# A down projection in seven half-size products with its split weight sums made beforehand

## The chip, the cores and the metric

The kernel runs on one NeuronCore of a Trainium2 chip. The metric is the time of one execution on the device in microseconds (us). The engines are TensorE (PE, with PEld for its weight loads), VectorE (DVE), ScalarE (ACT), GpSimd (POOL) and SyncE (SP). Here SP issues every transfer, in one queue in order.

## The reference, cut to what matters

One layer of a diffusion backbone for 128 context tokens and 2048 latent tokens, 2176 in all, with 1024 features, in float32. After a mixer (a gated short convolution and a bidirectional mLSTM) comes the feed-forward part, which the change concerns:

```
h2 = rmsnorm(x, norm2) * (1 + scale2) + shift2
up = conv3(h2 @ w_up)                  # 2 x 2816 features, 3 taps along the grid's columns
a, gg = split(up)
u = silu(gg) * a                       # 2816 features
x = x + gate2 * (u @ w_down)           # 2816 -> 1024
y = rmsnorm(x, final_norm)
```

D_FF is 2816 = 22 x 128. The gate and the shift differ between context and latent tokens.

## The kernel before

Features lie on the 128 partitions, tokens along the free dimension. Every float32 operand of a product is split into a high part (an ACT copy to the type that TensorE multiplies, `fp32r`) and a low part (the rest, a subtraction on DVE or POOL), and a product is three matmuls: high x high, high x low, low x high, into one PSUM bank.

The **mixer** goes over the second half of the tokens first (the blocks BB: heads, `shortconv`, heads), then over the first half (BA), where products of the projections fill the gaps of the mLSTM's units (`weave`). In it, `load_w` (L101) loads a weight block into one of two buffers, ACT makes its high part and POOL its low part; `gemm` (L191) is 24 matmuls of 384 or 256 columns into one of four accumulators.

The **up projection** already works by Strassen and Winograd's scheme: two halves of the tokens (`hf`), 22 units of features (`j`), and for each unit seven products of half size instead of eight (L918 on), with sums of tokens in seven slots (`sums`, `split`) and sums of weights made per unit (`weights`). `conv` (L879) follows one unit behind. It convolves the two raw results, multiplies them to `u` and stores 128 features of it in `uD` (L907).

The **down projection** is plain. For four groups of 544 tokens and eight blocks of 128 output features, 22 x 2 x 3 matmuls of 272 columns (L1030 to L1032) gather in two PSUM banks. `load_u` (L974) loads and splits the 22 pieces of u of a group, the next group's behind the last products of this one. `load_d` (L983) loads and splits the block's weights again in each group, the high part on ACT, the low part shared by POOL and DVE. `close` (L1034) adds the bank, scaled by the gate, onto the residual x. `finish` (L997) takes the squares' sums, gets their inverse roots by a small product and a power on POOL, spreads them over the partitions by another small product, scales the eight blocks and stores them.

A layer over the program sets the order of the instructions on each engine: it may put work that is ready ahead of work that stands earlier in the code, as far as buffers allow, and it makes all waits. On the chip each engine and SP's queue keep that order, so an instruction that waits holds up all behind it.

## Time and profile before

| what | value |
|---|---|
| executions | 2618.68, 2618.84, 2621.7 us; median 2618.84 |
| span of the profiled execution | 2622.1 us |
| mean granted clock of TensorE | 0.988 |
| PE busy | 2539.1 us, 97% |
| DVE / ACT / POOL busy | 1501.3 / 1066.1 / 706.4 us |
| moved by DMA | 403.25 MB, mean 154 GB/s |
| down projection, last up product to last down product | 2062.8 to 2610.5 us |

The profiled execution's time is its span here; no other time of it is given. A group's row in the profile has the line, engine and operation, what it writes and reads, the shape, the count, then busy time and mean duration of one, and the idle time ahead of it with what ended it. Matmuls overlap in the pipeline, so a mean duration is more than the distance between two starts. A row of the timeline has the start, the time it took, the engine, the line and the operation.

### The profile page before, as it was taken

The page shows a single profiled execution, that of the slowest core. Times are in us where ns is not written, and L with a number is a line of the kernel's source. Part 1 is how long each engine was busy: PE and PEld are TensorE (multiplying, and loading weights), DVE is VectorE, ACT ScalarE, POOL GpSimd, SP SyncE. Part 2 cuts the span into 40 slices and gives each one's busy share as a digit, 9 for nine tenths or more (in the row PEclk, how much of TensorE's full clock was granted, in tenths as well). Part 3 has the DMA queues.
Part 4 walks back from the last instruction along what each step waited for, and adds up shares of the span by engine and source line. Part 5 has one row for each costly group of instructions (what it writes and reads, how often), then busy time and mean ns, then how long its engine had stood idle before and what let it go on. Part 6 is the DMA issues. An engine that isn't in the chain of part 4 may idle for free. (4 is left out here: it accounts for less than half of the span.)

```text
span 2622.1 us, 46918 instructions
## 1 busy us (share of the span) xinstructions
PE 2539.1 (97%) x18511; PEld 2519.2 (96%) x18511; DVE 1501.3 (57%) x2560; ACT 1066.1 (41%) x2028; POOL 706.4 (27%) x534
## 2 busy tenths in 40 slices
PE   8999999999988988899999999999999999999998
PEld 7999999999988988899999999999999999999998
DVE  3993242333457666797686669666666635353533
ACT  4521142322345454464454446554544523232411
POOL 2542242211333344221121112111111222232232
PEclk9999999999999999999999999999999999999999
DMA  8773142555467887854252224222222635454442
GB/s 280 250 254 101 57 140 85 155 180 155 152 195 242 253 256 235 267 195 139 84 178 91 79 79 165 83 83 82 83 83 90 234 113 184 156 179 150 149 139 77
DMA packets 223582, 403.25 MB, mean 154 GB/s; under 512 B 20722, under 2 KB 144770, under 8 KB 221698
## 3 DMA queue, kind: packets, MB, share of 16 engines
q1 hardware_dynamic: 223362, 400.25, 46.5%
q8 instruction: 145, 2.38, 0.4%
q14 instruction: 75, 0.61, 0.1%
HBM read 305.13 MB, written 95.04 MB: 153 GB/s over the span
## 5 line engine op out<-in xcount | busy, mean ns | idle before, releaser
L196 PE MATMUL acc<-hH,wh 128*128 128x384 f32 (+1 forms) x1536 | 516.4, 336 | 0.0
L198 PE MATMUL acc<-hH,wl 128*128 128x384 f32 (+1 forms) x1536 | 505.0, 329 | 0.0
L197 PE MATMUL acc<-hL,wh 128*128 128x384 f32 (+1 forms) x1536 | 504.7, 329 | 0.0
L938 PE MATMUL pa<-tH,wh 128*128 128x272 f32 x1408 | 410.1, 291 | 5.6 <-DVE raw L950 5.2
L940 PE MATMUL pa<-tH,wl 128*128 128x272 f32 x1408 | 409.3, 291 | 0.4 <-DVE wl L276 0.4
L1030 PE MATMUL d<-uh,wh 128*128 128x272 f32 x1408 | 406.0, 288 | 3.1 <-ACT raw L948 3.1
L939 PE MATMUL pa<-tL,wh 128*128 128x272 f32 x1408 | 407.1, 289 | 0.0
L1032 PE MATMUL d<-uh,wl 128*128 128x272 f32 x1408 | 406.9, 289 | 0.0
L1031 PE MATMUL d<-ul,wh 128*128 128x272 f32 x1408 | 404.4, 287 | 0.0
L276 POOL TENSOR_TENSOR wl<-st,wh 128x512 fp32r<-128x512 f32 x132 | 182.3, 1381 | 730.5 <-ACT wh L275 697.5
L108 POOL TENSOR_TENSOR wl<-wst,wh 128x512 fp32r<-128x512 f32 (+1 forms) x160 | 234.3, 1486 | 434.0 <-ACT wh L105 421.5
L196 PEld LDWEIGHTS acc<-hH,wh 128*128 128x128 f32 x1536 | 291.1, 190 | 1.5 <-issue 0.4
L197 PEld LDWEIGHTS acc<-hL,wh 128*128 128x128 f32 x1536 | 291.1, 189 | 1.0
L198 PEld LDWEIGHTS acc<-hH,wl 128*128 128x128 f32 x1536 | 290.5, 189 | 0.2 <-issue 0.2
L938 PEld LDWEIGHTS pa<-tH,wh 128*128 128x128 f32 x1408 | 266.8, 190 | 6.4 <-issue 5.7
L1030 PEld LDWEIGHTS d<-uh,wh 128*128 128x128 f32 x1408 | 266.9, 190 | 3.4 <-ACT raw L948 3.3
L939 PEld LDWEIGHTS pa<-tL,wh 128*128 128x128 f32 x1408 | 267.3, 190 | 0.0
L940 PEld LDWEIGHTS pa<-tH,wl 128*128 128x128 f32 x1408 | 266.6, 189 | 0.6 <-DVE wl L276 0.6
L1032 PEld LDWEIGHTS d<-uh,wl 128*128 128x128 f32 x1408 | 266.1, 189 | 0.1
L1031 PEld LDWEIGHTS d<-ul,wh 128*128 128x128 f32 x1408 | 265.3, 188 | 0.0
L993 POOL TENSOR_TENSOR wl<-st,wh 128x704 fp32r<-128x704 f32 x64 | 150.5, 2352 | 367.2 <-ACT wh L991 358.2
L884 DVE SCALAR_TENSOR_TENSOR tt<-raw,fw,tt 128x127 f32<-128x127 f32 (+4 forms) x264 | 245.7, 959 | 1.5 <-ACT tt L890 0.8
(215 smaller groups left out, 5031.6 us busy)
## 6 DMA issues: line engine op xcount, KB each, us to landing
st<-in_w_up SPq DMA_DIRECT2D x88, 512.0 KB, 4.4
st<-in_w_down SPq DMA_DIRECT2D x64, 704.0 KB, 4.2
wst<-in_w_in SPq DMA_DIRECT2D x48, 512.0 KB, 4.1
us<-uD SPq DMA_DIRECT2D x88, 272.0 KB, 4.4
R<-nD SPq DMA_DIRECT2D x34, 512.0 KB, 5.5
wm<-in_w_modr SPq DMA_DIRECT2D x32, 512.0 KB, 4.7
F<-tD SPq DMA_DIRECT2D x12, 1088.0 KB, 8.8
uD<-tt SPq DMA_DIRECT2D x22, 576.0 KB, 2.8
```

What stands on the lines that cost most here:

```text
L108: G.tensor_sub(wl[:, a:a + n // 2], st[:, a:a + n // 2], wh[:, a:a + n // 2].bitcast(F32))
L196: PE.matmul(acc[:, :n], w_h, hH[:, k, :n], start=(k == 0), stop=False)
L197: PE.matmul(acc[:, :n], w_h, hL[:, k, :n], start=False, stop=False)
L198: PE.matmul(acc[:, :n], w_l, hH[:, k, :n], start=False, stop=(k == KT - 1))
L276: (G if on_pool else V).tensor_sub(wl, a, wh.bitcast(F32))
L884: V.scalar_tensor_tensor(o, i, w, o, op0=ALU.mult, op1=ALU.add)
L938: PE.matmul(acc, wh[:, w], rh, start=(kk == 0 and i in (0, 1, 5)), stop=False, skip_group_check=True)
L939: PE.matmul(acc, wh[:, w], rl, start=False, stop=False, skip_group_check=True)
L940: PE.matmul(acc, wl[:, w], rh, start=False, stop=(kk == 3), skip_group_check=True)
L1030: PE.matmul(acc[b][:, :NB], wh[:, c], uh[:, q], start=(j == 0), stop=False)
L1031: PE.matmul(acc[b][:, :NB], wh[:, c], ul[:, q], start=False, stop=False)
L1032: PE.matmul(acc[b][:, :NB], wl[:, c], uh[:, q], start=False, stop=(j == FT - 1))
```

## The change

1. **Down projection.** It too is made of seven products of half size. Tokens are taken in two halves of 1024 and 1152 (`HN`), features in three groups of 8, 8 and 6 blocks (`KS` pairs), outputs in four pairs of blocks (`mp`). That gives six "supers" (`SUP`) of 4 x 7 products, each with two quarters of columns (256 or 288). Each product needs one of seven sums of u, split into `uH` and `uL` (the slots `ds`, of 2048, 1536, 2304 or 1728 columns), and one of seven sums of weights, loaded as `wd` already split.
2. **Weight sums.** `prep_down`, 24 units of work run beside the mixer, loads w_down, makes the four sums and the seven splits of each unit and stores them in `wD` (168 parts, two output buffers `pw`). `wD` is read twice, once for each half of the tokens, through five buffers `wd`.
3. **Sums of u.** `conv` keeps the u of an even unit and, with that of the odd one, makes four sums and stores seven arrays in `uD`.
4. **Residual.** `evict` adds each product's bank at once onto the residual (`accs`), scaled by the gate. Since later products add onto the same bank, a bank is read between two products that add to it.
5. **Splits of u.** `Split` loads a sum into one of two buffers (`fd`), makes the high part on ACT and the low part on DVE. The seven splits of the next super go with the last pair of the present one.
6. **Final norm.** `finish` works on 1024 tokens of the first half and twice 576 of the second.

The diff, cut to its core (the old down projection, which it removes, is printed above):

```diff
+KS = (4, 4, 3)
+HN = (1024, 1152)
...
+    uD = [dr.tile([3, 7, P, 4, n // 2], F32, name=f"uD{i}") for i, n in enumerate(HN)]
+    wD = dr.tile([3, 4, 7, P, 2, 512], F32, name="wD")
...
+    def prep_down():
+        for mp in range(4):
+            for s in range(3):
+                for k0 in range(0, KS[s], 2):
+                    n = min(2, KS[s] - k0) * P
+                    c0 = (4 * s + k0) * P
+                    st = pp.tile([P, 2, 2, 256], F32, name="pst", bufs=2)
+                    Q.dma_start(st[:, :, :, :n], I["w_down"][mp][:, :, :, c0:c0 + n])
+                    a11, a12, a21, a22 = (st[:, m, k, :n] for m in range(2) for k in range(2))
+                    yield
...
+                    def part(i, a, on_pool=False):
+                        o = pp.tile([P, 2, 256], F32R, name="pw", bufs=2)
+                        S.activation(o[:, 0, :n], a, AF.Copy)
+                        (G if on_pool else V).tensor_sub(o[:, 1, :n], a, o[:, 0, :n].bitcast(F32))
+                        Q.dma_start(wD[s, mp, i][:, :, k0 * P:k0 * P + n], o[:, :, :n].bitcast(F32))
+                    part(0, a11)
+                    s1 = add(V.tensor_add, a21, a22, "ps1")
+                    part(1, s1)
+                    yield
...
+            store(4, b21)
+            store(5, b22)
+            yield
+            tt = up.tile([P, 4, 576], F32, name="ut")[:, :, :n // 2]
+            x = [tt[:, i].rearrange("p (q t) -> p q t", q=2) for i in range(4)]
+            V.tensor_sub(x[0], b12, b11)
+            V.tensor_sub(x[1], b22, x[0])
+            yield
+            V.tensor_sub(x[2], b22, b12)
+            V.tensor_sub(x[3], b21, x[1])
+            Q.dma_start(dst[:4].rearrange("i p t -> p i t"), tt)
...
+    slot_d(6)
+    fd = open_pool("fd", 2)
+    slot_d(0)
+    wd = open_pool("wd", 5)
+    for i in ORDER[2:]:
+        slot_d(i)
...
+    todo = [Split(0, 0, i) for i in ORDER]
+    for x in todo[:2]:
+        x.load()
+    ws = [next(loads) for _ in range(4)]
+    load_x(xa, 0, 0)
+    for k, x in enumerate(todo):
+        x.high()
+        x.low()
+        if k + 2 < 7:
+            todo[k + 2].load()
+        if k == 2:
+            next(cv, None)
+    run(cv)
+    phu.close()
+    xb = open_pool("xb", 8, "left")
+    dp = open_pool("dp", 1, "left")
+    for mp in range(1, 4):
+        load_x(xb, 0, mp)
...
+    def product(hf, s, mp, i, q, w):
+        N = HN[hf] // 4
+        kind = "ababaca"[i]
+        if i in (0, 1, 5):
+            banks[kind, q] = pu.tile([P, 512], F32, name="p" + kind, bufs=3 if kind == "a" else 2)
+        acc = banks[kind, q][:, :N]
+        th, tl = ds[ORDER[i]]
+        for kk in range(KS[s]):
+            c = slice((2 * kk + q) * N, (2 * kk + q + 1) * N)
+            k = slice(kk * P, (kk + 1) * P)
+            PE.matmul(acc, w[:, 0, k], th[:, c], start=(kk == 0 and i in (0, 1, 5)), stop=False, skip_group_check=True)
+            PE.matmul(acc, w[:, 0, k], tl[:, c], start=False, stop=False, skip_group_check=True)
+            PE.matmul(acc, w[:, 1, k], th[:, c], start=False, stop=(kk == KS[s] - 1), skip_group_check=True)
+        h, blk = DST[i]
+        evict(hf, mp + 4 * h, q, blk, acc)
...
+        for mp in range(4):
+            lows = []
+            for i in range(7):
+                ws.append(next(loads, None))
+                w = ws.pop(0)
+                for q in range(2):
+                    product(hf, s, mp, i, q, w)
+                for x in lows:
+                    x.low()
+                if lows:
+                    lows = []
+                    if i + 1 < 7:
+                        todo[i + 1].load()
+                if todo and mp == 3:
+                    todo[i].high()
+                    lows.append(todo[i])
+                elif todo and mp == 2 and i > 4:
+                    todo[i - 5].load()
```

Three places show how the instructions stand. The first is ACT in the short convolution of the second half of the tokens, where `cr` and `yr` are evictions and scalings of its products and `wh` the high part of the next weights. Before:

```order
L377 ACTIVATE yr<-cr,scw 128x384
L372 ACTIVATE cr<-acc 128x384
L105 ACTIVATE wh<-wst 128x1024
L372 ACTIVATE cr<-acc 128x256
L377 ACTIVATE yr<-cr,scw 128x256
```

and in the changed kernel, with the parts `pw` of the weight sums:

```order
L318 ACTIVATE pw<-pst 128x256
L413 ACTIVATE cr<-acc 128x384
L318 ACTIVATE pw<-ps_5243 128x256
L418 ACTIVATE yr<-cr,scw 128x384
L318 ACTIVATE pw<-ps_5296 128x256
L318 ACTIVATE pw<-ps_5302 128x256
L318 ACTIVATE pw<-ps_5362 128x256
L413 ACTIVATE cr<-acc 128x256
L106 ACTIVATE wh<-wst 128x1024
```

Between two evictions now stand two to five parts; 71 of the 168 stand in this convolution, most of the others in the heads and the values that follow it.

The second is SP's queue at the end of the up projection. Before (`us` is a piece of u, `ot` the residual, `st` weights):

```order
L988 DMA st_22499<-in_w_down 128x1408
L988 DMA st_22506<-in_w_down 128x1408
L976 DMA us_22513<-uD_73 128x544
L907 DMA uD_73<-tt_22265 128x1152
L976 DMA us_22519<-uD_73 128x544
```

and in the changed kernel (`acc` is the residual, `wd` a block of weight sums, `ut` the last sums of u):

```order
L1063 DMA us_23618<-uD0_73 128x2048
L1076 DMA wd_23604<-wD_75 128x1024
L1087 DMA acc_23612<-xD_70 128x1024
L1063 DMA us_23622<-uD0_73 128x2048
L1063 DMA us_23626<-uD0_73 128x2048
L981 DMA uD1_74<-ut_23651 128x4x576
L1063 DMA us_23633<-uD0_73 128x2048
L1063 DMA us_23637<-uD0_73 128x2048
L1087 DMA acc_23664<-xD_70 128x1024
L1087 DMA acc_23674<-xD_70 128x1024
L1076 DMA wd_23676<-wD_75 128x1024
```

Rows that only repeat are left out: four `wd` stand where the first one does, and six `acc` ahead of the last row, which loads the fifth block of weights.

The third is DVE at the end of the first super, where L1115 is an eviction (the old L1037) and L1070 a low part `uL` of the next super's sums (the old L980):

```order
L1115 SCALAR_TENSOR_TENSOR acc_23674<-pb_24329,modT_85,acc_23674 128x256
L1070 TENSOR_TENSOR uL_23560<-us_24262,uH_23559 128x2048
L1115 SCALAR_TENSOR_TENSOR acc_23674<-pb_24343,modT_85,acc_23674 128x256
L1115 SCALAR_TENSOR_TENSOR acc_23672<-pa_24297,modT_85,acc_23672 128x256
L1070 TENSOR_TENSOR uL_23568<-us_24293,uH_23567 128x2048
L1115 SCALAR_TENSOR_TENSOR acc_23672<-pa_24312,modT_85,acc_23672 128x256
L1070 TENSOR_TENSOR uL_23576<-us_24358,uH_23575 128x2048
```

An eviction now waits behind a low part, which waits for its load. The seven low parts spread over the last pair of this super and the first of the next.

281 lines of the change are left out of this document (163 added, 118 removed).

## The prediction

> **What bounds the kernel now.** I read the page's totals first, then the groups by line, then the starts of single products, and last the waits around the two places where the down projection begins and ends.
>
> ```profile
> span 2622.1 us, 46918 instructions
> PE 2539.1 (97%) x18511; PEld 2519.2 (96%) x18511; DVE 1501.3 (57%) x2560; ACT 1066.1 (41%) x2028; POOL 706.4 (27%) x534
> L1030 PE MATMUL d<-uh,wh 128*128 128x272 f32 x1408 | 406.0, 288 | 3.1 <-ACT raw L948 3.1
> L1031 PE MATMUL d<-ul,wh 128*128 128x272 f32 x1408 | 404.4, 287 | 0.0
> L1032 PE MATMUL d<-uh,wl 128*128 128x272 f32 x1408 | 406.9, 289 | 0.0
> ```
>
> TensorE is busy for 97% of the span, and the down projection is 3 x 1408 = 4224 products of 272 columns that hardly wait. Their 288 ns each overlap, so the price of one is the distance between two starts. Below stand the first and last row of four quiet stretches: a stretch of the down projection (82 rows listed), of the up projection (82), and of mixer products of 256 columns (36) and 384 columns (8).
>
> ```profile
> 2109.84 0.29 PE L1032 MATMUL d<-uh,wl 128*128 128x272 f32 x1
> 2119.92 0.29 PE L1032 MATMUL d<-uh,wl 128*128 128x272 f32 x1
> 1499.72 0.29 PE L939 MATMUL pa<-tL,wh 128*128 128x272 f32 x1
> 1509.93 0.29 PE L939 MATMUL pa<-tL,wh 128*128 128x272 f32 x1
> 317.82 0.28 PE L197 MATMUL acc<-hL,wh 128*128 128x256 f32 x1
> 322.00 0.29 PE L196 MATMUL acc<-hH,wh 128*128 128x256 f32 x1
> 304.73 0.34 PE L198 MATMUL acc<-hH,wl 128*128 128x384 f32 x1
> 305.97 0.34 PE L196 MATMUL acc<-hH,wh 128*128 128x384 f32 x1
> ```
>
> That is 10.08/81 = 0.1244 us a product in the down projection, 10.21/81 = 0.1260 in the up projection, 4.18/35 = 0.1194 at 256 columns and 1.24/7 = 0.177 at 384.
>
> **Term 1, the products.** Seven products of half size instead of eight leave 3696: 1848 of 256 columns (tokens 0 to 1023) and 1848 of 288. From 272 to 384 columns the price rises by (0.177 - 0.1244)/112 = 0.00047 a column, so 288 columns cost 0.132. Low: 1848 x (0.1194 + 0.132) = 465 us. High, with the up projection's dearer rate, since the new products stand in its pattern (0.1260/0.1244 = 1.013): 471. Before: 4224 x 0.1244 = 525.5. Saved: 55 to 61; taken 58.
>
> **Term 2, the final norms.** From the last up product to the last down product:
>
> ```profile
> 2062.78 0.29 PE L940 MATMUL pa<-tH,wl 128*128 128x272 f32 x1
> 2610.48 0.14 PE d L1032
> 2062.00:2064.00 2.00, 1.07 (x9) 1.00 0.89 269
> 2064.00:2066.00 2.00, 0.00 (x0) 0.80 0.87 279
> 2066.00:2068.00 2.00, 1.87 (x8) 0.50 0.78 287
> 2070.00:2072.00 2.00, 2.00 (x11) 0.50 0.90 306
> PE d L1030 <- ACT raw L948: 3.1, 1, 3.1
> PE st L133 <- POOL fr L126: 3.9, 8, 1.0
> ```
>
> The windows' columns are: length, PE busy, products, granted clock, DMA share, GB/s. The stretch is 547.7 us, 22 more than its products. The start takes 3.1 us of idle time plus some 6.8 us at clock 0.50, half of which is lost, together 6.6. The remaining 15 lie in the norms, eight of them (two blocks in each of four groups), each with sums, a power on POOL and a spreading product back to back. The change has four pieces for the kernel's body; the order shows 24 products between the two halves of the first, so POOL's answer is there in time. I leave 3 us for them: 12 saved (9 to 14).
>
> **Term 3, the start.** The old start loaded 272 KB pieces in the order of their use. The new one splits seven sums of 128x2048 in turn through two buffers, and SP has one queue. Rows for what a piece costs:
>
> ```profile
> L257 ACT ACTIVATE tH<-F x14: 1097/1112/1129, 1574.0 to 1605.9; 128x1088 fp32r<-128x1088 f32 x14
> L258 DVE TENSOR_TENSOR tL<-F,tH x14: 1278/1284/2377, 1575.3 to 1608.0; 128x1088 fp32r<-128x1088 f32 x14
> F<-tD SPq DMA_DIRECT2D x12, 1088.0 KB, 8.8
> 2050.00:2060.00 10.00, 10.00 (x81) 1.00 0.98 340
> 2230.00:2240.00 10.00, 10.00 (x83) 1.00 0.98 356
> L1037 DVE SCALAR_TENSOR_TENSOR ot<-d,modT,ot 128x272 f32<-128x272 f32 (+2 forms) x72 | 30.4, 464 | 156.6 <-PE d L1032 156.6
> ```
>
> At 2048 columns the high part costs 2.0 us on ACT and the low part 2.3 on DVE (from 1.11 and 1.28 at 1088, nearly in proportion). Full DMA engines move about 350 GB/s, so 1 MB of sums takes 3 us and its landing 5 to 9. Counting from the last up product as 0: DVE still has the last conv's taps, and the low parts 1 and 2 end near 5 and 7; the evictions of part 0 stand behind two more taps, near 11, and part 2 adds onto their bank. The multiply, three sums and the evictions of parts 1 and 2 follow to 16.5, and low parts 3 and 4 to 19 and 21. Only then are the sums 5 and 6 issued, whose buffers these free, and behind them on SP stand six loads of residual (3.1 MB) and then the fifth block of weights, issued near 24. With its own 0.5 MB, 5.7 MB have to move from 19 on, so it lands near 19 + 5.7/0.35 = 35. Parts 4, 5 and 6 follow it at 24 x 0.12 = 2.9 us each and end at 44 instead of 7 x 2.9 = 20. That is 24 us, less the 6.6 of before, about +18. Bounds: if the weights overtake, only the DVE chain is left, 12 - 6.6 = +5; with 3 us of half clock more, +22.
>
> **Term 4, five changes of token sums.** Each of the next five groups needs seven splits while TensorE works. The nearest row is the up projection's own change of halves, seven splits of about the same size in seven stages:
>
> ```profile
> 1590.00:1600.00 10.00, 9.59 (x77) 9.37 (x76) 9.06 (x11) 5.46 (x9) 1.23 (x1) 1.00 1.01 341
> 1600.00:1610.00 10.00, 9.12 (x71) 8.68 (x69) 9.89 (x12) 9.02 (x15) 2.05 (x1) 1.00 0.43 164
> 1610.00:1620.00 10.00, 8.00 (x61) 7.81 (x62) 10.00 (x17) 3.60 (x6) 3.79 (x3) 1.00 0.45 164
> 1400.00:1600.00 200.00, 199.59 (x1584) 199.37 (x1583) 142.57 (x220) 103.82 (x178) 38.38 (x27) 1.00 0.29 98
> ```
>
> Here 77 + 71 + 61 products stand where 3 x 82 would (the quiet rows above): 37 x 0.126 = 4.7 us lost. In the new phase DVE has less else to do (two evictions of 0.46 us in a step of 2.9), but a split waits for its own load, which waits for the low part two before it, and the order puts evictions behind low parts. A pair goes round in about 7 (landing) + 2.0 + 2.3 = 11.3 us against three steps of 2.9 = 8.7; three rounds fall 8 us behind, and the order has already set the last low parts into the next group's steps, which covers 4 to 6. I take 3.2 each: +16. Bounds 0 (cover holds) and 30 (the 4.7 and one landing later).
>
> **Term 5, the weight sums in the mixer.** Added: 24 loads of w_down, and 168 parts, each an ACT copy, a DVE subtraction and a store of 256 KB, plus 96 DVE sums. In all some 52 MB. The order moves most of it into the short convolution of the second half of the tokens, where the engines are idle:
>
> ```profile
> 260.00:320.00 60.00, 60.00 (x379) 60.00 (x378) 12.73 (x20) 9.83 (x15) 10.25 (x8) 1.00 0.19 60
> 320.00:380.00 60.00, 60.00 (x417) 60.00 (x416) 24.53 (x49) 30.12 (x64) 26.84 (x26) 1.00 0.45 145
> L239 ACT ACTIVATE tH<-F 128x272 fp32r<-128x272 f32 x12 | 5.0, 423 | 1.9 <-DVE F L233 1.7
> L240 DVE TENSOR_TENSOR tL<-F,tH 128x272 fp32r<-128x272 f32 x12 | 6.4, 530 | 0.0
> sD<-sb SPq DMA_DIRECT2D x32, 258.0 KB, 2.6
> xD<-row SPq DMA_DIRECT2D x40, 192.0 KB, 3.1
> ```
>
> Busy time there is no issue: 168 x 0.42 = 71 us on ACT, 264 x 0.53 = 140 on DVE, inside some 350 us. The two output buffers are: a part's buffer is free when its store has landed, so two parts take 0.42 + 0.53 + 0.2 (hand-overs) + 2.6 to 3.1, or 1.9 to 2.1 us a part. The order sets 71 parts beside 12 x (2 x 4.2 + 2.9) = 134 us of products, 1.9 us a part. At 2.1 the ACT, DVE and SP queues fall 71 x 0.24 = 17 us behind, and TensorE's evictions and weight loads stand in them; three free accumulators of 4.2 us cover 12. Taken +7; bounds 0 and the rival's +40.
>
> **Terms 6 and 7.** Sums of u: four subtractions of 512 or 576 columns per two units (0.68 us each at the rate of L258) add 2.7 us of DVE in the time of 2 x 168 products, 42 us, of which the last row of term 4's fence has it busy 142.57/200 = 71%; with the added stores, hidden but at the change of halves: +2 (0 to 6). The tail:
>
> ```profile
> 2611.70 0.45 DVE ss L1046
> 2615.27 0.50 DVE ot L1004
> 2616.17 2.45 DVE ot L1004 x6
> ```
>
> The last norm now covers 576 columns instead of 272 in two pieces through one bank: about 0.6 more for squares and sums, 2.5 for the second piece and the copy, 8 x 0.3 for the scalings, some shared with the store: +5 (2 to 7).
>
> **Sum** on the profiled span: 2622.1 - 58 - 12 + 18 + 16 + 7 + 2 + 5 = 2600. The median shown lies 3.3 us below the span: **2597 us**.
>
> **Rivals.** *A, everything hides:* weights overtake at the start (+5), changes cost nothing, mixer nothing: -58 - 12 + 5 + 0 + 0 + 0 + 4 = -61, 2558 us. For it: TensorE waits in the old down phase for norms alone once it has started. Against: the two-buffer round trip in term 4.
>
> *B, the mixer's stores set the pace (slower):* with 52 MB in some 350 us, 149 GB/s more, the DMA share goes from 0.19 to 0.45 up to 0.8 or so, and stores may land in 4 us instead of 2.6; then a part costs (0.42 + 0.53 + 0.2 + 4)/2 = 2.6, and 120 parts set at 1.9 to 2.1 us fall 0.6 x 120 = 70 us behind; less 12 at two places of cover, +46, i.e. 2600 + 39 = 2639 on the span, 2636 us. It makes the kernel slower from a landing of about 3.5 us on. For it: 192 KB already take 3.1. Against: 258 KB take 2.6, as the median of 32.
>
> *C, the new phase is bound by DMA:* it moves 81 MB of weights (each twice), 43 of sums, 18 of residual and output, 141 MB in 467 + 24 + 16 + 3 = 510 us, 276 GB/s. At a share of 0.98 the rows give 340 to 356, so on average it fits, at 0.8. At a mean of 250 GB/s it would take 564 us: +54, 2651 us, slower.
>
> *D, waits throttle the clock:* after the 3.1 us of idle at 2063 the clock stood at 0.50 for about 6.8 us. Were each of the five changes to do so, 5 x 3.4 = +17: 2614 us, no change. Against: the change of halves lost 4.7 us in pieces with the clock at 1.00. The Trainium skill (TensorE: Matmul & The Clock Gate, Part 1) says that an idle window of about 3.4 us throttles the array to half; the trace agrees at 2064 (0.50 in windows after an idle stretch of 3.06 us), and shorter waits here did not do it.
>
> **How the numbers follow.** Forecast 0.50 (2583 to 2612), A 0.22, B 0.13, C 0.07, D 0.08. This measurement cannot tell 0.2% (5 us) from no change, so faster means under 2613.6. Forecast and A are nearly all faster, D splits, B and C are slower but for small doses: faster 0.74, same 0.09, slower 0.17. The forecast's own range is 2583 to 2612; with A at 2558 below and the small doses of B above, 8 in 10 lie in 2560 to 2632.
>
> **What would show it.** Term 1: products 0.12 and 0.13 us apart and 3696 of them. Term 3: a wait of TensorE on the DMA of wd, 10 us or more, in the first group. Term 4: waits on evictions or uL near each group's end, 2 to 5 us. Term 5: the short convolution's window stays full (60 of 60) or not. Term 7: some 17 us after the last product instead of 11.6. I am wrong if the mixer stretches by over 20 us, or if the down phase is under 485 or over 535 us.

## The result, and the profile after

The changed kernel takes 2691.3 us (median of 4 runs, 2684.4 to 2694.2) where the kernel before takes 2620.3 on the same chip (4 runs, 2618.7 to 2626.3): a ratio of 1.0259, 95% interval 1.0238 to 1.0280. It is 2.6% slower; 2597 us had been forecast. Its profiled execution took 2689.7 us with a span of 2687.9.

The page after, its totals; then, from the list of starts, the first product of the up projection before and after, and the up projection's last product after:

```profile
span 2687.9 us, 46847 instructions
PE 2513.0 (93%) x17959; PEld 2480.9 (92%) x17959; DVE 1760.1 (65%) x3039; ACT 1062.9 (40%) x2077; POOL 569.8 (21%) x460
```

```profile
1114.02 0.57 PE L938 MATMUL pa<-tH,wh 128*128 128x272 f32 x1
```

```profile
1184.63 0.57 PE L1012 MATMUL pa<-tH,wh 128*128 128x272 f32 x1
2141.72 0.29 PE L1014 MATMUL pa<-tH,wl 128*128 128x272 f32 x1
```

TensorE has fewer products and is busy for 26 us less, in a span that is 66 us longer. These landmarks, with the last product of the kernel before at 2610.3, cut the span into four stretches:

| stretch | before | after | difference | forecast |
|---|---|---|---|---|
| mixer (to the first up product) | 1114.0 | 1184.6 | +70.6 | +7 |
| up projection | 948.8 | 957.1 | +8.3 | +2 |
| down phase (last up to last down product) | 547.5 | 521.5 | -26.0 | -36 |
| tail (to the end) | 11.8 | 24.7 | +12.9 | +5 |

So the part of the program that the change is about did get shorter, and what the mixer took longer is almost three times that gain.

**The mixer.** The same two windows that the prediction quoted for the short convolution, after the change (length; then busy time and count of PE, PEld, DVE, ACT and POOL; granted clock, DMA share, GB/s):

```profile
260.00:320.00 60.00, 53.45 (x339) 52.64 (x339) 29.78 (x68) 18.96 (x43) 8.13 (x6) 0.97 0.61 194
320.00:380.00 60.00, 57.35 (x348) 56.10 (x347) 29.36 (x57) 21.45 (x45) 16.02 (x12) 1.00 0.65 200
```

They held 379 and 417 products and were full; now they hold 339 and 348, in the second partly because the program stands up to 43 us later there. DVE and ACT are busy for no more than half of the time. The groups of the tile `pw` (the parts of the weight sums) say what these two engines do instead: the rows count the idle time that stood just before an instruction on `pw`, by what ended it.

```profile
L318 ACT ACTIVATE pw<-ps x96: 292/417/421, 148.8 to 625.9; 128x256 fp32r<-128x256 f32 x80, 128x128 fp32r<-128x128 f32 x16
  DMA wD<-pw: 221.6, 115
  ACT pw L318: 183.1, 95
DMA to landing us min/median/max: 2.1/2.9/5.5
```

ACT stood for 221.6 us ahead of 115 parts until the store of an earlier part had landed, and DVE for 183.1 us until ACT had made the part's high half. Neither is anyone's loss by itself, but the evictions of the mixer's products stand in the same two queues behind these waits. The largest waits of TensorE between 120 and 690 us (in all, times, longest):

```profile
PE acc L197 <- ACT row L389: 9.7, 7, 4.4
PE acc L197 <- DVE cr L416: 9.1, 4, 3.6
PE st L134 <- DVE xt L172: 7.9, 2, 4.2
```

All of them there come to 48.5 us, against 4.0 before. Some 22 are for an accumulator that was not yet emptied, most of the others for work of DVE and ACT that stands in the same queues, as the norm's `xt` and the mLSTM's gates.

**The start of the down phase.** The windows after the last up product, TensorE's wait there, and SP's rows:

```profile
2140.00:2150.00 10.00, 8.26 (x64) 7.64 (x63) 8.49 (x5) 6.41 (x6) 0.00 (x0) 1.00 0.99 344
2150.00:2160.00 10.00, 5.20 (x27) 4.82 (x27) 9.64 (x15) 4.99 (x3) 0.00 (x0) 0.82 0.89 337
2160.00:2170.00 10.00, 4.28 (x22) 4.08 (x22) 5.31 (x4) 3.82 (x2) 0.00 (x0) 0.67 0.94 355
2170.00:2180.00 10.00, 2.87 (x13) 2.90 (x14) 2.29 (x1) 0.00 (x0) 0.00 (x0) 0.50 1.03 413
```

```profile
2177.13 0.55 PE L1165 MATMUL pa<-uH,wd 128*128 128x256 f32 x1 [12.85 <-DMA wd<-wD]
```

```profile
2162.47 3.13 SPq L1087 DMA_DIRECT2D acc<-xD  x6
2165.64 16.37 SPq L1076 DMA_DIRECT2D wd<-wD  x6
```

The fifth block of weights is issued at 2165.64, 23.9 us after the last up product and straight behind the six residual loads; TensorE gets it 35.4 us after that product. The four windows hold 126 products where 4 x 83.4 would stand: 207 x 0.12 = 25 us lost.

**The changes of token sums, and one stall more.** A window of 10 us holds 83.4 products of 256 columns or 75.4 of 288. The five changes, and between the third and the fourth of them one window that is none:

```profile
2240.00:2260.00 20.00, 18.00 (x148) 17.65 (x148) 14.44 (x19) 7.66 (x4) 0.00 (x0) 1.00 0.88 330
2330.00:2340.00 10.00, 8.88 (x73) 8.53 (x72) 7.44 (x13) 2.97 (x2) 0.00 (x0) 1.00 0.91 322
2390.00:2410.00 20.00, 17.32 (x132) 16.72 (x132) 16.30 (x20) 10.89 (x7) 1.01 (x1) 1.00 0.83 295
2420.00:2440.00 20.00, 14.19 (x91) 13.95 (x91) 11.92 (x16) 0.00 (x0) 0.00 (x0) 0.83 0.97 348
2500.00:2520.00 20.00, 17.64 (x132) 17.23 (x131) 12.68 (x14) 6.39 (x3) 0.00 (x0) 1.00 0.88 339
2590.00:2600.00 10.00, 8.09 (x60) 7.69 (x59) 6.58 (x9) 3.30 (x2) 0.00 (x0) 1.00 0.94 319
```

The changes lose about 2.3 + 1.3 + 3.4 + 2.5 + 2.0 = 11.5 us with the clock at 1.00. The fourth row, a group already begun, loses 60 x 0.1326 = 7.9. There DVE's eviction waits for the second half's residual, and SP shows why that came late:

```profile
2434.39 0.94 DVE L1115 SCALAR_TENSOR_TENSOR acc<-pa,modT,acc 128x288 f32<-128x288 f32 x2 [4.87 <-DMA acc<-xD]
```

```profile
2420.00 7.49 SPq L1147 DMA_DIRECT2D out_y<-acc  x6
2427.58 1.89 SPq L1087 DMA_DIRECT2D acc<-xD  x2
```

Six output stores of the first half, each waiting for its scaling on DVE, stand ahead of the two loads.

**The tail.** From the last product on (starts on TensorE, ACT and DVE):

```profile
2663.22 0.29 PE L1167 MATMUL pa<-uH,us 128*128 128x288 f32 x1
```

```profile
2667.30 0.68 ACT L1129 ACTIVATE sq<-acc 128x576 f32<-128x576 f32 x1 [7.33 <-DVE acc L1146]
```

```profile
2665.67 1.54 DVE L1146 SCALAR_TENSOR_TENSOR acc<-acc,nrm,sq 128x576 f32<-128x576 f32 x2
2678.67 5.92 DVE L1146 SCALAR_TENSOR_TENSOR acc<-acc,nrm,sq 128x576 f32<-128x576 f32 x8 [1.66 <-ACT sq L1140]
```

The last squares wait until 2667.30 for the scalings of the *first* 576 columns, because the row of inverse roots that these read lies in the one buffer `sq` that the squares write.

### The profile page after: what moved, and what is told of

Its sections match the earlier page's. It is cut to its first block, busy times and chain, and to the rows that moved or that the text cites. A ratio compares the mean times of both kernels' runs of the same rounds, so it can differ in the third digit from the quotient of the medians.

```text
span 2687.9 us, 46847 instructions
## 1 busy us (share of the span) xinstructions
PE 2513.0 (93%) x17959; PEld 2480.9 (92%) x17959; DVE 1760.1 (65%) x3039; ACT 1062.9 (40%) x2077; POOL 569.8 (21%) x460
## 5 line engine op out<-in xcount | busy, mean ns | idle before, releaser
L197 PE MATMUL acc<-hH,wh 128*128 128x384 f32 (+1 forms) x1536 | 523.4, 341 | 22.0 <-ACT row L389 9.7
L277 POOL TENSOR_TENSOR wl<-st,wh 128x512 fp32r<-128x512 f32 x132 | 201.3, 1528 | 715.8 <-ACT wh L276 589.5
L1165 PE MATMUL pa<-uH,wd 128*128 128x256 f32 (+1 forms) x698 | 204.9, 294 | 27.8 <-DMA wd<-wD 15.9
L1066 ACT ACTIVATE uH<-us 128x2048 fp32r<-128x2048 f32 (+3 forms) x42 | 78.4, 1869 | 337.9 <-PE pa L1167 238.7
L1167 PE MATMUL pa<-uH,wd 128*128 128x256 f32 (+1 forms) x698 | 204.0, 292 | 0.0
L1014 PE MATMUL pb<-tH,wl 128*128 128x272 f32 x704 | 203.9, 290 | 0.0
L1166 PE MATMUL pa<-uL,wd 128*128 128x256 f32 (+1 forms) x698 | 203.9, 292 | 0.0
L1012 PE MATMUL pb<-tH,wh 128*128 128x272 f32 x704 | 203.7, 289 | 0.0
L1013 PE MATMUL pb<-tL,wh 128*128 128x272 f32 x704 | 202.8, 288 | 0.0
```

What stands on the lines that cost most here:

```text
L197: PE.matmul(acc[:, :n], w_h, hH[:, k, :n], start=(k == 0), stop=False)
L277: (G if on_pool else V).tensor_sub(wl, a, wh.bitcast(F32))
L1012: PE.matmul(acc, wh[:, w], rh, start=(kk == 0 and i in (0, 1, 5)), stop=False, skip_group_check=True)
L1013: PE.matmul(acc, wh[:, w], rl, start=False, stop=False, skip_group_check=True)
L1014: PE.matmul(acc, wl[:, w], rh, start=False, stop=(kk == 3), skip_group_check=True)
L1165: PE.matmul(acc, w[:, 0, k], th[:, c], start=(kk == 0 and i in (0, 1, 5)), stop=False, skip_group_check=True)
```

## The experiments

The first product of the up projection says what a kernel did to the mixer. It scatters between profiles: in the seven kernels whose mixer has no weight sums it comes at 1105 to 1114 us (mean 1110), in the four with the changed kernel's mixer at 1175 to 1185 (mean 1178). Differences under 10 us are not read from it. The down phase, where it is left as in the changed kernel, scatters from 516 to 529 (mean 524).

All runs together; "down" and "tail" as in the table above, times are medians, kernel before 2619 to 2622 in all of them:

| run | first up product | up | down | tail | us | ratio, 95% interval |
|---|---|---|---|---|---|---|
| changed kernel | 1184.6 | 957.1 | 521.5 | 24.7 | 2691.3 | 1.0238 to 1.0280 |
| e1 no parts | 1105.2 | 955.6 | 528.0 | 24.7 | 2621.8 | 0.9995 to 1.0027 |
| e2 parts without stores | 1147.0 | 957.6 | 527.9 | 24.7 | 2659.2 | 1.0134 to 1.0173 |
| e3 stores without parts | 1139.8 | 955.9 | 524.4 | 24.7 | 2646.6 | 1.0085 to 1.0125 |
| e4 four buffers | 1167.0 | 955.4 | 521.7 | 24.6 | 2672.7 | 1.0182 to 1.0252 |
| e5 parts later | 1190.7 | 955.5 | 524.3 | 24.7 | 2699.0 | 1.0274 to 1.0344 |
| e6 parts in the up projection | 1107.7 | 1078.9 | 527.5 | 24.7 | 2740.8 | 1.0422 to 1.0519 |
| e7 three edits behind it | 1175.4 | 956.8 | 518.0 | 24.6 | 2682.9 | 1.0205 to 1.0286 |
| e8 no sums of u | 1176.6 | 952.7 | 516.0 | 24.7 | 2675.6 | 1.0184 to 1.0266 |
| e9 dealt out, four buffers | 1125.3 | 957.3 | 528.7 | 24.7 | 2635.2 | 1.0027 to 1.0066 |
| e10 parts in the down phase | 1108.9 | 957.2 | 536.7 | 25.8 | 2630.7 | 1.0024 to 1.0052 |
| e11 e10 and residual loads | 1114.1 | 957.9 | 527.3 | 25.8 | 2626.1 | 0.9999 to 1.0030 |
| e12 e11 and last norm | 1107.3 | 957.6 | 529.8 | 20.8 | 2618.3 | 0.9977 to 1.0007 |
| e13 dealt out, two buffers | 1157.1 | 955.6 | 523.1 | 25.2 | 2662.1 | 1.0135 to 1.0172 |
| e14 third buffer for sums | 1177.1 | 953.8 | 553.5 | 24.7 | 2709.7 | 1.0302 to 1.0353 |
| e15 joined, with e14's buffers | 1128.1 | 955.3 | 547.1 | 20.0 | 2646.5 | 1.0076 to 1.0113 |
| e16 joined, without them | 1122.4 | 956.0 | 515.2 | 20.0 | 2615.1 | 0.9972 to 0.9995 |
| e17 e12, low parts shared | 1111.8 | 955.6 | 541.7 | 20.8 | 2635.9 | 1.0050 to 1.0088 |
| e18 e16, dealt out wider | 1142.2 | 954.9 | 513.7 | 20.8 | 2632.7 | 1.0032 to 1.0067 |

### What the parts cost, taken apart (e1, e2, e3)

```diff
 # e1
-            pd_ = prep_down()
+            pd_ = iter(())
...
-        Q.dma_start(t.bitcast(F32), wD[s, mp, i][:, :, :n])
+        Q.dma_start(t.bitcast(F32), uD[0][s, i][:, :2, :n])
 # e2: the second of these edits, and in part()
-                        Q.dma_start(wD[s, mp, i][:, :, k0 * P:k0 * P + n], o[:, :, :n].bitcast(F32))
 # e3: in part(), no sums
-                        o = pp.tile([P, 2, 256], F32R, name="pw", bufs=2)
-                        S.activation(o[:, 0, :n], a, AF.Copy)
...
+                        Q.dma_start(wD[s, mp, i][:, :, k0 * P:k0 * P + n], st[:, i % 2, :, :n])
```

> Leaves out all making of weight sums in the mixer (no w_down loads, no parts, no stores); the down projection loads blocks of the same size and shape from stored sums of u instead, so it multiplies by the wrong numbers, in the same time. My theory (the parts and their stores cost the mixer its +70 us): first up product back near 1114 us and 2690 - 70 = 2620 us. Rival (the changed pools or the order around them slow the mixer, not the parts): first up product stays near 1185 and the time near 2690.

> Makes every part (168 ACT copies, 264 DVE sums and differences, 24 loads) but leaves out their 168 stores; the down projection loads blocks of the same size from stored sums of u, so its numbers are wrong. Theory L (ACT and DVE stand still until a store has landed and frees a buffer): the instructions alone cost little, first up product at 1114 to 1125, 2620 to 2632 us. Rival E (the instructions themselves, 71 us of ACT and 140 of DVE ahead of evictions): first up product above 1165, 2670 us or more. Rival Q (the bytes and SP's queue): as L.

> Keeps the 24 loads of w_down and the 168 stores of the same bytes, straight from the loaded tile, and leaves out all arithmetic of the parts, so the weight sums are raw weights. Theory L: no ACT or DVE instruction waits for a store any more, first up product at 1114 to 1130, 2620 to 2637 us. Rival Q (44 MB of stores in SP's queue and in the DMA engines hold up the mixer's own loads): first up product above 1160, 2665 us or more. Rival E: as L.

Without the parts the mixer is back at 1105 and the kernel at 2621.8: the parts are the whole loss. Of the 68 us (1178 against 1110), the parts' arithmetic without stores takes 37 and the stores without arithmetic 30; each of the two runs has the 24 loads of w_down as well. None of the three theories had that: L expected almost nothing from either half, E all from the first, Q all from the second.

TensorE's waits between 120 and 560 us in e2 name the queues, with the longest single wait in the last column:

```profile
PE acc L197 <- ACT row L388: 10.4, 7, 4.8
PE acc L197 <- DVE cr L415: 6.3, 5, 2.1
PE acc L197 <- ACT cr L412: 5.8, 5, 2.1
```

`row` and `cr` are evictions: no accumulator is free since ACT and DVE are at parts or wait for what a part needs. Without stores little holds the parts back, and all 168 stand in 195 us. In e3 the other resource is full. Its window of the short convolution, and ACT's wait for the mixer's own weights between 120 and 560 us (four waits, one of 19.2 us; in e1 the four come to 12.3):

```profile
205.00:360.00 155.00, 139.47 (x858) 138.13 (x857) 32.29 (x47) 26.11 (x38) 31.38 (x24) 0.94 0.90 292
```

```profile
ACT wh L106 <- DMA wst<-in_w_in: 60.9, 4, 19.2
```

The order differs between these kernels, so 37 + 30 = 67 shows that both kinds of work cost, not that they add in general.

### Buffers, and where the parts stand (e4, e5, e9, e13)

```diff
 # e4 (the four sums of a group share one tile, for room)
-                        o = pp.tile([P, 2, 256], F32R, name="pw", bufs=2)
+                        o = pp.tile([P, 2, 256], F32R, name="pw", bufs=4)
 # e5
-                run(islice(go, 4), pd_)
+                run(islice(go, 4), pd_ if b > 0 else None)
 # e9 (four buffers) and e13 (two): one or two parts per step of the generator, and
 # each step is queued on ACT behind an eviction
+    def beat(ins):
+        with tc.issue_after(ins.ins):
+            next(PD[0], None)
...
-            S.activation(r[:, :n], acc[:, :n], func, scale=scale)
+            at = S.activation(r[:, :n], acc[:, :n], func, scale=scale)
+            beat(at)
```

> All work as in the changed kernel, but four output buffers for the parts instead of two (the four sums of a group share one tile to make room). A part then costs (0.42 + 0.53 + 0.2 + 2.9)/4 = 1.0 us at most from its buffers. Theory L: over half of the 70 us comes back, first up product below 1150, 2655 us or less. Rivals E and Q: nothing changes, 2680 us or more.

> The whole changed kernel, but the first parts are made one block of tokens later, so that the order no longer sets a dozen of them beside the modulation's products on DVE (between 150 and 205 us DVE is busy 49 of 50 us there). Theory M (an ACT part that waits for DVE or for its load holds up the evictions behind it where DVE is full, and that stretch costs 19 of the 79 us): first up product at 1160 to 1170 us, 2666 to 2676 us. Rival (the loss moves along with the parts): first up product at 1180 or later, 2686 us or more.

> All work of the changed kernel, four output buffers for the parts as in the earlier run with four, and the parts dealt out: one or two parts are queued on ACT behind each eviction of the mixer, instead of bursts of two to five, so that the last of them lie in the second half of the mixer. Theory O (it is bursts of parts between two evictions in ACT's and DVE's queues that TensorE waits for): first up product at 1135 or earlier, 2635 to 2650 us. Rival W (every part costs TensorE its share wherever it stands): as with four buffers, first up product near 1167 and 2673 us.

> The parts dealt out as in the run before (one or two behind each eviction of the mixer), but with the two output buffers of the changed kernel. Theory O (bursts in the queues are the whole loss): as with four buffers, first up product at 1120 to 1132, 2630 to 2643 us. Rival L (stores that land late hold ACT even so; both edits are needed): first up product at 1140 to 1165, 2650 to 2675 us.

Two more buffers alone bring the first up product from 1178 to 1167, dealing out alone to 1157, both together to 1125 (and 1128 and 1122 in two kernels built on it): 11, 21 and 53 of the 68 us. In the medians of the whole kernel the three are 19, 29 and 56 us, so that both together bring more than their sum is likely but not sure. The idle time ahead of parts that ended with a store's landing, in e4, e13 and e9:

```profile
  DMA wD<-pw: 72.5, 53
```

```profile
  DMA wD<-pw: 120.9, 77
```

```profile
  DMA wD<-pw: 8.8, 7
```

No run but the pair of e13 and e9 changes one thing alone. In e4 the shared tile made parts wait 57.5 us for their sums, and the order set them closer, into 328 us instead of 484. e13 and e9 also load w_down one group ahead, begin behind the modulation and set fewer parts in the convolution. So the next table shows where the time goes. It cuts the mixer at the first eviction `cr` of the convolution, the first eviction `row` after it and the first product of the mLSTM's sums. A cell has the us lost against the kernel before and, in brackets, the parts that start there. In the kernels without parts or stores in the mixer the cells lie between -5 and +3.

| run | ahead of the convolution | in it | from it to the mLSTM's sums | later |
|---|---|---|---|---|
| changed kernel | 18.9 (13) | 23.8 (71) | 20.8 (58) | 7.1 (26) |
| e2 parts without stores | 26.3 (29) | 12.5 (139) | -4.5 (0) | -1.3 (0) |
| e3 stores without parts | 5.7 | 21.9 | 0.4 | -2.2 |
| e4 four buffers | 23.0 (18) | 26.5 (102) | 9.9 (48) | -6.3 (0) |
| e5 parts later | 21.6 (11) | 23.0 (71) | 25.5 (56) | 6.7 (30) |
| e13 dealt out, two buffers | 3.8 (0) | -1.3 (40) | 24.3 (71) | 16.4 (57) |
| e9 dealt out, four buffers | 4.8 (0) | -3.4 (40) | 7.2 (74) | 2.7 (54) |

e13 and e9 set their parts in nearly the same places and differ in buffers alone. Up to the end of the convolution neither loses more than 5 us; behind it the two buffers cost 31 us more, and TensorE waits there mostly for DVE's work on the mLSTM, hardly for evictions. Theory O, bursts alone, therefore falls with e13. Theory L, landing alone, does not fit e4, which waits a third as long for landings and loses no less up to the end of the convolution. Dealt out, the convolution is full or nearly so with either number of buffers (TensorE is busy for 153.66 and 155.00 of the 155 us from 205 to 360, against 142.20 in the changed kernel); whether that is due to the order or to 40 parts in place of 71 was not tested apart.

The stretch ahead of the convolution is another matter. Between 145 and 205 us DVE computes the modulation; before, after, and e9, whose first part comes at 210:

```profile
145.00:205.00 60.00, 60.00 (x376) 60.00 (x375) 57.35 (x96) 10.96 (x20) 22.76 (x11) 1.00 0.66 208
```

```profile
145.00:205.00 60.00, 51.62 (x311) 50.13 (x310) 59.05 (x106) 11.78 (x26) 16.21 (x9) 0.97 0.85 274
```

```profile
145.00:205.00 60.00, 60.00 (x377) 59.74 (x376) 58.78 (x94) 11.10 (x19) 22.77 (x12) 1.00 0.71 239
```

Twenty-six ACT instructions stand there instead of twenty, on a DVE that was full already, and 65 products are gone. e5, whose first part comes at 193 instead of 145, gained nothing (1190.7), and it lost its 21.6 us in this same stretch, which again held 311 products. ACT's rows show why, first of the changed kernel, then of e5:

```profile
203.91 0.42 ACT L318 ACTIVATE pw<-pst 128x256 fp32r<-128x256 f32 x1 [12.71 <-DMA pst<-in_w_down]
192.75 0.42 ACT L318 ACTIVATE pw<-pst 128x256 fp32r<-128x256 f32 x1 [13.25 <-DMA pst<-in_w_down]
```

A part stands ahead of evictions in ACT's queue and waits 13 us for its load of w_down; in e5 SP issues that load only at 185.3, among the modulation's weights, which wait for DVE. So e5 moved the first parts but not this wait, and theory M, which names it, is not refuted: these rows speak for it. In e2, too, 26 of the 37 us stand in this stretch. e9 and e13 lose 4 to 5 us there. No run moves the load alone.

### Other places for the parts (e6, e10)

```diff
 # e6: a generator like e9's, stepped in the loop of the up projection
+            if hf or j > 1:
+                with tc.issue_after(mark.ins):
+                    next(pd_, None)
...
+                        S.activation(o[:, 0], a, AF.Copy)
+                        G.tensor_sub(o[:, 1], a, o[:, 0].bitcast(F32))
 # e10: no wD; the parts are made two products ahead in the down projection
+    def quarter(s, mp, m, k):
+        t = wd.tile([P, 512], F32, name=f"a{m}{k}")[:, :KS[s] * P]
+        Q.dma_start(t, I["w_down"][mp][:, m, k, 4 * s * P:(4 * s + KS[s]) * P])
...
+                S.activation(t[:, 0], x, AF.Copy)
+                (G if i in (0, 5, 6) else V).tensor_sub(t[:, 1], x, t[:, 0].bitcast(F32))
```

> All weight sums are made during the up projection instead of the mixer, in pieces of 128 columns (308 parts), two parts per 3.1 us, each step queued on ACT behind an eviction; sums and low parts on POOL instead of DVE. Theory (it is the mixer's full queues, not the work, that make the parts dear): first up product at 1105, the up projection 957 + 5 to 15, in all 2621 + 5 to 15 = 2626 to 2636 us. Rival (the work is dear wherever it stands, since ACT waits for stores and POOL's weights come late): up projection at 990 or more, 2655 us or more.

> No weight sums in the mixer and none stored: the down projection loads the raw quarters of w_down and makes the seven parts two products ahead, as the up projection does (per pair of output blocks 7 ACT copies, 4 DVE sums, 4 low parts on DVE and 3 on POOL; 24 MB of weights instead of 52 stored and loaded 81). Theory (without the detour over DRAM the parts fit beside the products): first up product at 1105, down phase 525 to 540, in all 2619 to 2635 us. Rival W: low parts and sums stand before evictions there too, down phase at 560 or more, 2655 us or more.

In the up projection the parts cost 1079 - 957 = 122 us, more than in the mixer: the rival had the size right. They are 308 smaller ones there (little SBUF is free), with three buffers and one for the load. The first row is idle time ahead of a part, the second the time that the up projection's own low parts on DVE waited for a part:

```profile
  DMA wD<-pw: 144.0, 100
  DVE wl L277: 39.9, 10
```

So dealing out alone did not make them cheap here; that the short buffers are the reason was not tested. In the down projection the parts need no store, and there the theory held: 536.7 us, 8 to 9 more than e1, and 2630.7 in all.

### The start, the residual, the tail and the sums of u (e7, e8, e11, e12, e14)

```diff
 # e7 and e11: residual pair by pair (e7 also loads a fifth block of weights ahead)
-    for mp in range(1, 4):
-        load_x(xb, 0, mp)
...
+                if not u and mp < 3 and i == 2:
+                    load_x(xb, 0, mp + 1)
 # e7 and e11: the next half's residual ahead of most stores
-    XL = {(0, 6): (xa, 1, 1), (1, 3): (xb, 1, 2), (1, 6): (xb, 1, 3)}
+    XL = {(0, 4): (xa, 1, 1), (1, 3): (xb, 1, 2), (1, 6): (xb, 1, 3)}
 # e12: a buffer of its own for the first piece's roots; its last scalings behind the last squares
+            fin = finish(1, 0, 576, fd.tile([P, 2304], F32, name="us"))
 # e8: a constant tile is stored in place of the four subtractions
-            V.tensor_sub(x[0], b12, b11)
...
 # e14
-    fd = open_pool("fd", 2)
+    fd = open_pool("fd", 3)
-    wd = open_pool("wd", 5)
+    wd = open_pool("wd", 3)
```

> The changed kernel with three edits behind the up projection: the fifth block of weights is loaded ahead and the six residual loads come one pair at a time (start); the next half's residual is loaded ahead of most of the first half's output stores (change of halves); the last norm is cut by finished blocks, so that 288 columns instead of 576 are left behind the last product (tail). Theory: the start loses 13 to 16 us instead of 25.7, the stretch 2420 to 2440 loses 0 to 3 instead of 8.6, the tail takes 12 to 17 us instead of 24.7: 2691 - 25 to -33 = 2658 to 2666 us. Rival (at the start the chain of splits on DVE ends last, not the weights; the norms of the last half stand on DVE whatever the cut): 2680 us or more.

> Leaves out the four subtractions of u per two units and stores a constant tile of the same bytes in their place, so the down projection's numbers are wrong. Theory (the subtractions take DVE from 142 to 160 of 200 us, and its queue is what TensorE waits for in places): up projection back from 957 to 949 to 951, 2683 to 2686 us. Rival (the added stores or the placing of buffers cost the 8 us): up projection stays at 955 or more, 2690 us.

> The kernel of the run above (parts in the down projection) with the residual loads at the start dealt out pair by pair, and the next half's residual loaded ahead of most output stores. Theory: the start gains 7 to 12 us as weights no longer stand behind the residual, the change of halves up to 8: 10 to 20 us less than the run above, 2605 to 2620 us. Rival (the chain of splits on DVE sets the start): within 4 us of the run above.

> The kernel of the run above and the last norm in another order: the first piece's remaining scalings come after the last piece's squares and sums, in the time in which DVE waits for the inverse roots, and both roots of the last piece are taken before they are spread. Theory: the tail falls from 24.7 to 16 to 19 us, 6 to 8 us less than the run above, 2598 to 2614 us, faster than the kernel before. Rival (DVE's scalings end last in any order): tail at 22 or more.

> The changed kernel with three buffers for the token sums on their way to be split, and three instead of five for the weights, which makes room. Theory (terms 3 and 4: the round trip of a sum through two buffers, some 11 us, is what the start and the five changes wait for): the start loses 8 to 14 us less, each change under 1 us instead of 2 to 4, down phase at 500 to 508 instead of 521, 2670 to 2678 us. Rival (evictions that stand behind low parts on DVE, and the last conv's taps at the start, set the pace; or weights three deep now come late): down phase at 518 or more, 2687 us or more.

e7: its first 40 us of the down phase hold 180 products instead of 122, 58 x 0.12 = 7 us gained, and the window of the residual's stall 71 instead of 35. Together that is near 12 us, but the phase is only 3.5 us shorter, within its scatter: the rest was lost again at other changes of token sums, where the order fell differently. The tail did not move: cut into 288 columns twice, the two norms stand one behind the other on the chain. Two of the three edits worked in their place and one was a miss, and the median came to 2682.9, where 2658 to 2666 had been expected and the rival had said 2680 or more.

e8: without the subtractions DVE is busy 143 of 200 us again, and the up projection takes 952.7 against 954 to 958 in the other kernels with sums of u (e6 apart): some 3 us, at most half of the +8.3. The rest came with the added stores or with where the tiles lie; no run separates these, and e8's stores, whose constant tile is ready from the start, ran earlier (280 GB/s in its first 100 us of up projection against 191).

e11 gains 9.4 us in the down phase against e10 but 4.5 in the median: less than the 10 to 20 that were expected, and hardly more than the scatter. e12's tail falls from 25.8 to 20.8, 5 us where 6 to 8 were expected, and the median by 7.8 to that of the kernel before, not below it as expected. In e16, which has the same order in its tail and its last product at 2593.58, the last scalings still take their 5.9 us on DVE:

```profile
2604.34 5.92 DVE L1159 SCALAR_TENSOR_TENSOR acc<-acc,nrm,sq 128x576 f32<-128x576 f32 x8 [3.95 <-ACT sq L1153]
```

e14 was to test the round trip of a sum through two buffers. The largest waits of TensorE in its down phase are these:

```profile
PE pa L1165 <- DMA wd<-wD: 33.0, 15, 10.1
PE pc L1165 <- DMA wd<-wD: 12.9, 5, 3.2
```

The waits for `uL` (3.3 us in the changed kernel) are gone, but 52 us of waiting for weights took their place: two blocks ahead, 5.8 us of products, were too few here, where the loads of sums stand in the same queue of SP. Whether the third buffer alone would shorten the changes stays open: there is no room for it beside five blocks of weights.

### All together (e15, e16, e17, e18)

e15 is e9 with e14's buffers, the residual loads and the last norm in the new order; e16 the same with the changed kernel's buffers. e17 is e12 with a quarter of each sum's low part on POOL, e18 is e16 with a group's parts behind five evictions instead of four and some in the mixer's second half.

> Parts dealt out with four buffers, three buffers for the token sums, the residual loads at the start pair by pair, the next half's residual ahead of most stores, and the last norm's scalings in the new order. If the parts add: 2635 - 13 to -21 (third buffer) - 4 (residual) - 8 (tail) = 2602 to 2610 us, faster than the kernel before. If the third buffer brings nothing: 2620 to 2626 us, no change.

> Parts dealt out with four buffers, five blocks of weights and two sums in flight as in the changed kernel, the residual at the start pair by pair, the next half's residual ahead of most stores, the last norm in the new order. If the gains add: 2635 - 4 (residual) - 8 (tail) = 2618 to 2627 us, no change against the kernel before.

> The kernel with the parts made in the down projection and both mends (2618 us), and a quarter of each sum's low part on POOL, which makes a low part 1.7 instead of 2.3 to 2.5 us on DVE. Theory (evictions stand behind low parts on DVE at the changes of token sums): down phase 530 falls to 518 to 526, 2606 to 2614 us. Rival (POOL's share of a sum takes longer than DVE's, and POOL makes the weights' low parts too): down phase at 530 or more, 2618 us or more.

> As the first of these three, but a group's seven parts go behind five evictions instead of four, and the second half of the mixer's output products take some too. Theory O (fewer parts between two evictions): first up product from 1125 to 1112 to 1120, 2608 to 2620 us. Rival (the second half of the mixer is full already): first up product at 1125 or later.

e15 takes over e14's loss (547.1). e16 comes to 2615.1 us, 3 below the range that adding its pieces gave. Against the changed kernel it is 76 us faster; against the kernel before its ratio is 0.9984 (0.9972 to 0.9995), less than the 0.2% that the prediction called the least that can be told. e17's POOL share costs 12 us of down phase instead of saving 4 to 12. e18's mixer reaches the mLSTM's outputs at 696.9 as e16 does (697.8), and then loses 20 us in the second half, which was the rival's place.

## Why the prediction was wrong, point by point

**Term 5 (weight sums in the mixer, +7) is the step that failed**: +70.6 between the two profiles, 68 between the means. Three things in it were wrong.

- *Cover was read from one stage.* The sum was made for the short convolution. The table above puts +18.9 us ahead of it, +23.8 in it, +20.8 between it and the mLSTM's sums and +7.1 later. Ahead of it DVE was busy for 57.35 of 60 us before, which the prediction never looked at, and the first parts waited there for their loads, a term that it did not have.
- *The price was nearly right, the cover not.* From the measured rows the buffers give (0.42 + 0.43 + 0.2 + 2.9)/2 = 2.0 us a part, and 71 parts in a convolution of 157 us went at a pace of 2.2, against the 2.1 that was named as the high price. The forecast then set "three free accumulators of 4.2 us cover 12" against a lag of 17. In the trace the convolution alone came out 23.8 us longer, so no cover shows. A reading that fits, though no run tests it, is that the forecast counted cover as if it were paid once into a smooth flow: at 2.2 us each, two to five parts make ACT late by 4 to 11 us between two evictions, again and again.
- *Engines that are idle on average were taken as room.* "Busy time there is no issue" held (DVE 29 to 30 of 60 us); what counted was what stood ahead of an eviction in the queue. e9 does the same work in the mixer with 15 us of loss.

**Rival B** had the sign and the queues right but the wrong cause and size: it needed stores that land in 4 us and gave 2636. They landed in 2.9 us (median), under its threshold of 3.5, and it was slower still. In e9 they land in 4.2 and the mixer is 53 us shorter.

**Term 1 (products, -58) was right.** First and last row of two quiet stretches, of 87 and 79 products:

```profile
2289.78 0.28 PE L1165 MATMUL pa<-uH,wd 128*128 128x256 f32 x1
2300.10 0.28 PE L1167 MATMUL pb<-uH,wd 128*128 128x256 f32 x1
...
2539.81 0.30 PE L1165 MATMUL pc<-uH,wd 128*128 128x288 f32 x1
2550.15 0.30 PE L1165 MATMUL pb<-uH,wd 128*128 128x288 f32 x1
```

10.32/86 = 0.1200 and 10.34/78 = 0.1326, against 0.1194 and 0.132: 1848 x 0.2526 = 467 us, inside 465 to 471.

**Term 2 (norms, -12)** was right for TensorE's own pieces, of which no wait in the body shows; but the first half's norm now holds up SP, and 7.9 us came back at 2420 to 2440 us. This stall was not foreseen. At the start the prediction had asked which loads stand behind others in SP's queue; it did not ask the same for the output stores.

**Term 3 (start, +18) was right in mechanism and size**: issue at 23.9 us (forecast: near 24), weights at 35.4 (35), 25 us lost (24). A wait of TensorE on `wd` of 10 us or more had been named as its sign; it is 12.85. The clock is at 0.50 in the window from 2170 to 2180 us. The Trainium skill (TensorE: Matmul & The Clock Gate, Part 1) has an idle stretch of about 3.4 us throttle the array; the wait of 12.85 us agrees. Shorter waits in the same start did it as well: after 2.48 us (ended at 2152.11) and 2.60 us (ended at 2159.91) products came 0.21 us apart instead of 0.12, and windows of 2 us from 2154 and from 2160 show the clock at 0.50. So the prediction's remark under rival D that shorter waits did not do it does not hold here. At the five changes no wait was longer than 1.7 us, and the clock stayed at 1.00.

**Term 4 (five changes, +16)** came to 11.5, inside its bounds of 0 to 30. That the two-buffer round trip sets it is not shown (e14).

**Term 6 (sums of u, +2)** was mis-sized: +8.3, of which the subtractions make at most half (e8). DVE's load was somewhat under-priced: 13 us in 200 by the prediction's sum, 18 by e8 against the changed kernel (143.03 and 160.82). The place was right in part. Counted from the first up product, five of nine stretches of 100 us hold as many products as before, so there the work was hidden as forecast. Missing are 21 products in the first 100 us, which the forecast did not have, and 50 in the 200 us around the change of halves, which it named; e8 gets back those of the first half of these 200 us alone. That half, before and after (length, PE busy, products, clock, DMA share, GB/s):

```profile
1514.02:1614.02 100.00, 97.71 (x769) 1.00 0.38 129
1584.63:1684.63 100.00, 97.22 (x748) 0.97 0.42 141
```

**Term 7 (tail, +5)** was mis-sized: +12.9. The scalings were priced right, at 0.3 us more each (5.92/8 = 0.74 against 2.45/6 = 0.41). What the sum lacked are the first piece's scalings, for which the last squares wait through the shared buffer: e12 took 5 us out there. The other 3 us, in the two pieces' small products and roots, were not tested by themselves.

**The other rivals.** A (everything hides) fell with the mixer. C (DMA-bound) did not happen: in the down phase a mean of 272 GB/s (2260 to 2560 us) goes with a share of 0.77. D (throttling at the changes) did not happen at the five changes; the stall at 2420 to 2440, with a mean clock of 0.83, is none of them. Of the two signs set for being wrong, the mixer stretched by over 20 us; the down phase, 521.5, stayed within 485 to 535.

## What to carry to other kernels

Side work put on engines that also empty the accumulators is priced by what stands in their queues ahead of an eviction, not by their idle share. Deal it out one or two pieces per eviction, load its input early enough that no piece waits for it, and give it so many output buffers that none waits for a landing; here buffers alone brought 11 us of 68, dealing out with earlier loads 21, all together 53. Read the cover in every stage in which the order places the work, and for each queue (SP's too) ask which loads stand behind an instruction that waits. A saving of 58 us of products is soon spent: the same scheme, laid out with care, came out 0.16% below the kernel before.

## What the runs showed of the hardware that had not been expected

- The landing time of the stores, most of them 256 KB, was a median of 2.9 us with two buffers in the changed kernel and 3.1 in e13, and 3.9 and 4.2 with four (e4, e9), with a least of 2.1 to 2.2 in all; e18, with four buffers and the parts dealt wider, has 2.9 again. The Trainium skill (DMA: Bandwidth & Descriptors, Latency and other measured facts) puts a fixed cost of some 2 us per transfer down mostly to the receipt from memory, growing with the load; the least of 2.1, which has the moving of the bytes in it, is of that size, and the 128 KB stores of e6 have a median of 2.2. So in e9 each store was slower than in the changed kernel and the kernel faster.
- Stores that nothing holds back can nearly fill the DMA engines: in e3, beside the mixer's own traffic, these stood at a share of 0.90 with 292 GB/s over 155 us, and ACT waited up to 19.2 us for a weight block of the mixer (3.6 in e1). In the changed kernel the share was 0.61 to 0.65 in the convolution.
- A subtraction of 128x128 on POOL took 0.45 us at best and up to 3.9 us (e6), on the engine that also makes low parts of TensorE's weights.
